# Inverse of the 16-blocks in a two-layer trunk: DRAM trips moved from the SP queue to Pool's queue, forward substitution moved from VectorE to Pool

## The chip, the cores and the metric

The kernel runs on one core of one Trainium2 chip. The metric is the device time of one execution in microseconds (us). PE is TensorE, DVE is VectorE, ACT is ScalarE, POOL is GpSimd, SP is SyncE; SPq is the queue of DMAs that SP issues. Every engine works its own list of instructions in the order in which the program wrote them.

## The reference

Two layers, each of three sub-layers on 256 rows of width 1024: a SwiGLU feed-forward, a token-mixing sub-layer, a second SwiGLU feed-forward, each with shift, scale and gate from a conditioning vector. The mixing sub-layer runs a convolution module, causal attention of 6 heads and a gated DeltaNet of 6 heads side by side. Everything is float32.

What matters here is in the DeltaNet: for each head and each chunk of 64 rows a unit lower triangular system is solved.

```
L = jnp.where(strict, jnp.einsum('bhncd,bhnsd->bhncs', k_beta, k) * decay, 0.0)
T = lax.linalg.triangular_solve(eye + L, jnp.broadcast_to(eye, L.shape), left_side=True, lower=True)
u = T @ v_beta
w = T @ (k_beta * jnp.exp(g)[..., None])
```

## The kernel before

**Weights.** All weights (about 250 MB) stream through four 1 MB buffers called `raw`, loaded by SP in a fixed order (`dmas`, line 420). ACT casts each unit to a high part `hi`, DVE subtracts to get a low part `lo` (`convert`, line 503), and PE multiplies in three passes. The conditioning matrix is accumulated on DVE (`adaacc`, `Lb`).

**What sets the order.** Each engine's list is written at build time by a planner: the class `Clock` (line 80) keeps a modelled time for each engine and for the DMA queue, and generators in `sides` (line 1655) step forward from `tick` when their inputs should be ready on PE's modelled time. So a change of what runs where also changes the order of other work.

**The mixing sub-layer.** PE multiplies the projection units in turn: rotated queries and keys (`mqk`, banks copied to `Y` tiles), attention values (`mv`, 48 matmuls of 384 columns), the gate `gz`. Between them stand the matmuls of the side work: the DeltaNet's products (`PT`, `LD`), attention scores and softmax (`E`), and the inverse.

**The inverse** (`inverse`, line 1367) takes the diagonal 32-blocks of the 24 chunk matrices in `LD`. SP writes them to DRAM (`scr_l`, line 1266, four DMAs) and reads the 16-blocks back with one block per partition (`Lb`, line 1378, two DMAs), so that 96 partitions hold 48 pairs. DVE then does 15 steps of forward substitution, two instructions each (`T` and `W`, lines 1389 and 1391), and a transposing copy (line 1392). SP writes the result to DRAM (`scr_w`, line 1398, four DMAs) and reads it back in the layout for PE (`C`, tile `Wc`, line 1400, two DMAs). PE combines the 16-blocks to 32-blocks and then 64-blocks in a chain of small matmuls, each followed by copies on ACT or DVE (lines 1410 to 1480). The DeltaNet (`delta_rule`) needs the end of that chain.

**The taps.** The depthwise convolution has 31 taps for each of two blocks, 62 in a mixing. A tap is either one DVE instruction (`cacc<-hc,colB,cacc`) or an ACT multiplication into one of two `ctap` buffers and an addition on Pool (`cacc<-cacc,ctap`). `taps` (line 1522) chooses by the modelled times; while `cfg["lo_pool"]` is false, which is from line 1372 to line 1393, it uses DVE alone. `fill` (line 1514) puts taps into modelled holes of DVE.

`idle("gp")` (line 1067) is a condition for a side generator: it waits until Pool's modelled time is close to PE's.

Of the kernel before, what the change touches and what calls it, by code (L numbers as in the profile page):

```python
# [14 lines left out]
OP = mybir.AluOpType  # L15
# [64 lines left out]
class Clock:  # L80


    def __init__(self):
        self.t = dict(pe=0.0, act=0.0, dve=0.0, gp=0.0, dma=0.0)
        self.writes, self.reads, self.used, self.slots, self.free = {}, {}, {}, {}, {}
        self.table = None
        self.filler = None
# [45 lines left out]
    def note(self, engine, op, args, kw):  # L133
        if op == "preload_act_table_set":
            self.t["act"] += 1.28 if args[0] != self.table else 0.0
            self.table = args[0]
            return
        out = kw.get("out", args[0] if args else None)
        ins = [x for x in list(args[0 if "out" in kw else 1:]) + [v for k, v in kw.items() if k not in ("out", "accum_out")]
               if hasattr(x, "tensor")]  # L140
        name = out.tensor.name
        start = max([self.t[engine], self.free.get(name, 0.0), self.last(self.reads, out), engine != "dma" and self.ready(out)]
                    + [self.ready(x) + 0.1 for x in ins])
        filler = self.filler
        if engine == "dve" and filler:
            self.filler = None
            while start - self.t["dve"] > HOLE and filler():
                pass
            self.filler = filler
            start = max(start, self.t["dve"])  # L150
        if engine == "dma":
            n = self.size(out) * out.shape[0] * 4 / 360e3
            self.t["dma"] = start + n
            end = start + n + (4.5 if "scr_" in name + ins[0].tensor.name else 2.0)
        else:
            end = self.t[engine] = start + self.cost(engine, op, out, ins)
        for log, aps in ((self.writes, [out, kw.get("accum_out", out)]), (self.reads, ins)):
            for x in aps:
                lo, hi = (0, 1 << 40) if engine == "dma" and x is out else self.span(x)
                w = log.setdefault(x.tensor.name, [])  # L160
                w[:] = [y for y in w if not (lo <= y[0] and y[1] <= hi)] + [(lo, hi, end)]
                self.used[x.tensor.name] = max(self.used.get(x.tensor.name, 0.0), end)
# [15 lines left out]
def trunk(ctx, tc, t, out):  # L178
    nc = tc.nc
# [1 line left out]
    psum = ctx.enter_context(tc.tile_pool(name="ps", bufs=1, space=PSUM))  # L181
    ctx.enter_context(tc.manual_schedule())
    clock = Clock()
    act, dve, pe, gp, sp = (clock.engine(n, e) for n, e in (("act", nc.scalar), ("dve", nc.vector), ("pe", nc.tensor),
                                                            ("gp", nc.gpsimd), ("dma", nc.sync)))

    def sb(shape, tag, dt=F32, bufs=1):
        return clock.tile(tag, bufs, pool.tile(shape, dt, name=tag, tag=tag, bufs=bufs))
# [67 lines left out]
    p = ps([128, 128], "x")  # L256
# [749 lines left out]
    scr_l = nc.dram_tensor("scr_l", [12, 4, 32, 32], F32, kind="Internal").ap()  # L1006
    scr_w = nc.dram_tensor("scr_w", [2, 12, 4, 32, 32], F32, kind="Internal").ap()
    late = {}

    def mixing(l, G, normed, nxt):  # L1010
# [128 lines left out]
        LD = LT[:, :NH * 256].rearrange("p (h t x) -> p h t x", t=2, x=128)  # L1139
# [117 lines left out]
        def pairs():  # L1257
            yield from until("kh")
            for h in range(NH):
                yield from until(("decay", h))  # L1260
                yield (kh, PT[:, h])
                yield from products(h, kh)
            yield (LD,)
            for q in range(4):
                c = slice(32 * q, 32 * q + 32)
                sp.dma_start(out=scr_l.rearrange("g b j i -> b j g i")[q], in_=LD.rearrange("p h t x -> p (h t) x")[c, :, c])
            ev["LT"] = True
            yield from until("qh")
            for h in range(NH):
                yield (qh,)  # L1270
                yield from products(h, qh)
            ev["PT"] = True
# [84 lines left out]
        W = sb([96, 2, 16, 16], "W")  # L1357
# [9 lines left out]
        def inverse():  # L1367
# [7 lines left out]
            Um, X = (buf[:, o:o + 384].rearrange("p (m i) -> p m i", i=32) for o in (256, 640))  # L1375
            for i in range(2):
                c = slice(16 * i, 16 * i + 16)
                sp.dma_start(out=Lb[48 * i:48 * i + 48], in_=scr_l.rearrange("h b j i -> (h b) j i")[:, c, c])
            yield (LD,)
            LM = LD.rearrange("p h t x -> p (h t) x")  # L1380
            for q in QUAD:
# [2 lines left out]
            V = W[:, 0]  # L1384
            for j in range(15):
                n, ni = j + 1, 15 - j
                T = sb([96, 64], "T", bufs=2)
                T = T[:, :n * ni].rearrange("p (c i) -> p c i", i=ni)
                dve.tensor_tensor(T, V[:, 0:n, j:j + 1].to_broadcast([96, n, ni]),
                                 Lb[:, j:j + 1, n:16].to_broadcast([96, n, ni]), op=OP.mult)  # L1390
                dve.tensor_tensor(V[:, 0:n, n:16], V[:, 0:n, n:16], T, op=OP.subtract)
            dve.tensor_copy(W[:, 1], V.rearrange("p c i -> p i c"))
            cfg["lo_pool"] = True
            C = sb([128, 2, 12, 32], "Wc")
            for f in range(2):
                for i in range(2):
                    c = slice(16 * i, 16 * i + 16)
                    sp.dma_start(out=scr_w[f].rearrange("h b c i -> (h b) c i")[:, c, c], in_=W[48 * i:48 * i + 48, f])
            for f in (1, 0):
                sp.dma_start(out=C[:, f], in_=scr_w[f].rearrange("h b c i -> (b c) h i"))  # L1400
            yield from until("kh")
            wide = sb([128, 1536], "S6a")
            TA, X64 = (wide[:, o:o + 768].rearrange("p (m i) -> p m i", i=64) for o in (0, 768))
# [533 lines left out]
    for n, (l, ph) in enumerate(order):  # L1937
        nxt = None
        if n + 1 < len(order):
            nl, nph = order[n + 1]  # L1940
            nxt = ((nl, 3 * nph + 1), (nl, 3 * nph))

        def normed(after=(), scaled=False, norm=True, l=l, ph=ph, n=n, G=G):
            if n and norm:
                rstd()
            h = modulate_whole(G["gs"], need_mod(l, 3 * ph), after) if ph == 1 else \
                modulate(G["gs"], need_mod(l, 3 * ph), after, scaled)
            if n == 0:
                cfg["wide"] = ("x", "x")
            cfg["lo_pool"] = True  # L1950
            cfg["mixing"] = ph == 1
            return h

        if ph == 1:
            G = mixing(l, G, normed, nxt)
        else:
            G = ffn(l, 1 if ph == 0 else 2, G, normed, 2 if ph == 0 else 8, nxt)
        if n == 0:
            zero = sb([128, 384], "E", bufs=3)
            gp.memset(zero, 0.0)  # L1960
            for f in range(2):
                sp.dma_start(out=scr_w[f].rearrange("h b c i -> (h b c i)").rearrange("(p n) -> p n", n=384), in_=zero)
            dve.tensor_copy(negdb, late["neg"][:, 0])
            dve.tensor_copy(negsb, late["neg"][:, 1])
            dve.tensor_copy(gt, late["neg"][:, 2])
            side_dma.append(load_rows(1))
# [23 lines left out]
```

## Time and profile before

| | us |
|---|---|
| three runs | 1217.0, 1206.73, 1216.96 |
| median | 1216.96 |
| profiled execution, own time | 1213.49 |
| its span | 1211.7 |
| PE busy | 1139.0 (94%) |
| DVE busy | 895.1 (74%) |
| ACT busy | 621.0 (51%) |
| POOL busy | 132.9 (11%) |

The profiled execution is one run with the hardware profiler; its span is what the trace covers. Busy times do not count DMA issue or waits. The granted clock is given as a share of the full 2.4 GHz. The two mixings stand at about 235 to 440 us (layer 0) and 830 to 1010 us (layer 1).

### The profile page before, as it was taken

The numbers are of one execution on the slowest core, as the hardware profiler recorded it, in microseconds if no ns is written. First come the engines' busy times: TensorE is split into PE (matmuls) and PEld (weight loads), VectorE is DVE, ScalarE is ACT, GpSimd is POOL, SyncE is SP. The second block draws the span as 40 slices with busy tenths as digits, with TensorE's granted clock in tenths as the row PEclk, the third lists the DMA queues.
The fourth block names the chain that finished last, engine by engine and source line by source line (L and its number), as shares of the span: only waits on it lengthen the run. The fifth ranks groups of instructions, "written<-read, shape, count | busy, mean of one in ns | idle before, by whom it ended". The sixth has DMA issues, their size and how long they took to land.

```text
span 1211.7 us, 22081 instructions
## 1 busy us (share of the span) xinstructions
PE 1139.0 (94%) x9085; PEld 1060.6 (88%) x9085; DVE 895.1 (74%) x1364; ACT 621.0 (51%) x1061; POOL 132.9 (11%) x139
## 2 busy tenths in 40 slices
PE   5799999999798779999999999999989989999997
PEld 4799999878677779999999999997868779999996
DVE  5778877658886588878769887774879938866554
ACT  4364444447646455444446544444656656544443
POOL 0610000102420010000001000001027101000001
PEclk9899999999879889999999999999988989999999
DMA  8759888656261376979764997893543514786640
GB/s 318 243 197 327 310 297 316 178 169 192 58 205 37 108 240 216 322 262 338 256 229 166 328 323 257 294 295 93 174 149 72 176 56 154 260 262 224 178 155 35
DMA packets 185740, 256.52 MB, mean 212 GB/s; under 512 B 26704, under 2 KB 152744, under 8 KB 185640
## 3 DMA queue, kind: packets, MB, share of 16 engines
q1 hardware_dynamic: 185640, 255.12, 63.1%
q8 instruction: 71, 1.16, 0.4%
q14 instruction: 29, 0.24, 0.1%
HBM read 252.86 MB, written 2.23 MB: 211 GB/s over the span
## 4 chain that ended last, share of the span: by engine, by line
PE 74%; DVE 16%; ACT 6%; issue 2%; POOL 1%; DMA 1%; SPq 0%; POOLq 0%; ACTq 0%; DVEq 0%
PE pm L171 45%; PE pa L171 27%; DVE adaacc L171 3%; DVE lo L171 2%; DVE H L171 2%; PE px L171 2%; ACT hi L171 1%; DVE W L171 1%; DVE v L171 1%; ACT L171 1%; DVE T L171 1%; DVE cacc L171 1%; DVE tmp L171 1%; DVE mod L171 1%; DMA xin_LT<-in_x_dram 1%
## 5 line engine op out<-in xcount | busy, mean ns | idle before, releaser
L171 PE MATMUL pm<-H,hi 128*128 128x256 f32 x2816 | 505.8, 282 | 1.4 <-DVE H L171 1.2
L171 DVE TENSOR_TENSOR lo<-raw,hi 128x1024 fp32r<-128x1024 f32 (+1 forms) x300 | 361.7, 1227 | 109.8 <-ACT hi L171 109.6
L171 PEld LDWEIGHTS pm<-H,hi 128*128 128x128 f32 x2816 | 431.9, 189 | 4.0 <-DVE H L171 2.0
L171 ACT CAST hi<-raw 128x1024 fp32r<-128x1024 f32 (+1 forms) x306 | 312.3, 1042 | 211.0 <-PE pm L171 93.8
L171 PE MATMUL pm<-H,lo 128*128 128x256 f32 x1408 | 392.5, 281 | 1.3 <-DVE lo L171 1.3
L171 PEld LDWEIGHTS pm<-H,lo 128*128 128x128 f32 x1408 | 264.7, 189 | 1.7 <-DVE lo L171 1.7
L171 PE MATMUL pa<-Y,hi 128*128 128x256 f32 x1312 | 245.7, 290 | 11.9 <-ACT S3a L171 7.5
L171 PEld LDWEIGHTS pa<-Y,hi 128*128 128x128 f32 x1312 | 208.3, 196 | 14.8 <-ACT S3a L171 7.9
L171 PE MATMUL pa<-Y,lo 128*128 128x256 f32 x656 | 187.8, 286 | 0.0
L171 PEld LDWEIGHTS pa<-Y,lo 128*128 128x128 f32 x656 | 129.5, 197 | 0.0
L171 ACT CAST Y<-tmp 128x256 fp32r<-128x256 f32 x88 | 35.9, 408 | 131.5 <-DVE tmp L171 131.5
L171 POOL TENSOR_TENSOR xin_LT<-xin_LT 128x256 f32<-128x256 f32 x35 | 27.1, 774 | 648.7 <-ACT xin_LT L171 646.4
L171 DVE SCALAR_TENSOR_TENSOR adaacc<-raw,c_act,adaacc 128x1024 f32<-128x1024 f32 x70 | 93.9, 1342 | 1.6
L171 POOL TENSOR_TENSOR cacc<-cacc,ctap 128x256 f32<-128x256 f32 x68 | 60.5, 890 | 204.8 <-DVE cacc L171 155.8
L171 DVE SCALAR_TENSOR_TENSOR Lb<-raw,c_act,Lb 128x1024 f32<-128x1024 f32 x56 | 71.8, 1283 | 4.3 <-DMA raw<-in_w_ada_dram 3.1
L171 DVE TENSOR_TENSOR Y<-tmp,Y 128x256 fp32r<-128x256 f32 x88 | 37.5, 426 | 41.7 <-ACT Y L171 41.7
L171 PE MATMUL pm<-Y,raw 128*128 128x256 f32 x288 | 66.8, 384 | 0.0
L171 PEld LDWEIGHTS pm<-Y,raw 128*128 128x128 f32 x288 | 53.4, 190 | 8.9 <-issue 1.0
L171 ACT ACTIVATE tmp<-pm 128x256 f32<-128x256 f32 x84 | 31.8, 379 | 52.1 <-PE pm L171 52.0
L171 PE MATMUL pa<-hi,Y 128*128 128x512 f32 x176 | 54.8, 393 | 0.0
L171 DVE TENSOR_REDUCE mod<-px 128x4 f32<-128x512 f32 x34 | 23.4, 689 | 33.6 <-PE px L171 33.5
L171 ACT ACT_TABLE_LOAD x28 | 35.9, 1283 | 14.9 <-DVE v L171 13.8
(301 smaller groups left out, 1337.8 us busy)
## 6 DMA issues: line engine op xcount, KB each, us to landing
raw<-in_w_ada_dram SPq DMA_DIRECT2D x70, 1024.0 KB
raw<-in_ffn_w_gate_dram SPq DMA_DIRECT2D x44, 1024.0 KB
raw<-in_ffn_w_up_dram SPq DMA_DIRECT2D x44, 1024.0 KB
raw<-in_ffn_w_down_dram SPq DMA_DIRECT2D x44, 1024.0 KB
raw<-in_w_in_dram SPq DMA_DIRECT2D x12, 1024.0 KB
raw<-in_w_in_dram SPq DMA_DIRECT2D x20, 512.0 KB
raw<-in_w_out_dram SPq DMA_DIRECT2D x16, 512.0 KB
raw<-in_w_in_dram SPq DMA_DIRECT2D x4, 768.0 KB
```

Source lines behind the costliest of these rows:

```text
L171: return getattr(real, op)(*args, **kw)
```

## The change

All 12 DMAs of each inverse go from SP's list to Pool's list (`qd` is a second modelled queue whose DMAs are issued by Pool), and so do the two DMAs that once write zeros to `scr_w` after the first sub-layer. The 30 instructions of the substitution and the copy go from DVE to Pool, with a yield on `idle("gp")` after each step. The planner has a modelled time `dma2` for Pool's DMAs beside Pool's own `gp`.

```diff
-        self.t = dict(pe=0.0, act=0.0, dve=0.0, gp=0.0, dma=0.0)
+        self.t = dict(pe=0.0, act=0.0, dve=0.0, gp=0.0, dma=0.0, dma2=0.0)
...
-        if engine == "dma":
+        if engine.startswith("dma"):
             n = self.size(out) * out.shape[0] * 4 / 360e3
-            self.t["dma"] = start + n
+            self.t[engine] = start + n
             end = start + n + (4.5 if "scr_" in name + ins[0].tensor.name else 2.0)
...
-                sp.dma_start(out=scr_l.rearrange("g b j i -> b j g i")[q], in_=LD.rearrange("p h t x -> p (h t) x")[c, :, c])
+                qd.dma_start(out=scr_l.rearrange("g b j i -> b j g i")[q], in_=LD.rearrange("p h t x -> p (h t) x")[c, :, c])
...
-                sp.dma_start(out=Lb[48 * i:48 * i + 48], in_=scr_l.rearrange("h b j i -> (h b) j i")[:, c, c])
+                qd.dma_start(out=Lb[48 * i:48 * i + 48], in_=scr_l.rearrange("h b j i -> (h b) j i")[:, c, c])
...
-                dve.tensor_tensor(T, V[:, 0:n, j:j + 1].to_broadcast([96, n, ni]),
+                gp.tensor_tensor(T, V[:, 0:n, j:j + 1].to_broadcast([96, n, ni]),
                                  Lb[:, j:j + 1, n:16].to_broadcast([96, n, ni]), op=OP.mult)
-                dve.tensor_tensor(V[:, 0:n, n:16], V[:, 0:n, n:16], T, op=OP.subtract)
-            dve.tensor_copy(W[:, 1], V.rearrange("p c i -> p i c"))
+                gp.tensor_tensor(V[:, 0:n, n:16], V[:, 0:n, n:16], T, op=OP.subtract)
+                yield idle("gp")
+            gp.tensor_copy(W[:, 1], V.rearrange("p c i -> p i c"))
...
-                    sp.dma_start(out=scr_w[f].rearrange("h b c i -> (h b) c i")[:, c, c], in_=W[48 * i:48 * i + 48, f])
+                    qd.dma_start(out=scr_w[f].rearrange("h b c i -> (h b) c i")[:, c, c], in_=W[48 * i:48 * i + 48, f])
             for f in (1, 0):
-                sp.dma_start(out=C[:, f], in_=scr_w[f].rearrange("h b c i -> (b c) h i"))
+                qd.dma_start(out=C[:, f], in_=scr_w[f].rearrange("h b c i -> (b c) h i"))
...
-                sp.dma_start(out=scr_w[f].rearrange("h b c i -> (h b c i)").rearrange("(p n) -> p n", n=384), in_=zero)
+                qd.dma_start(out=scr_w[f].rearrange("h b c i -> (h b c i)").rearrange("(p n) -> p n", n=384), in_=zero)
```

The order of the instructions, at the places on which the prediction rests (layer 0; layer 1 reads alike):

Pool's list from the zero fill to the start of the substitution, as the difference:

```order
 L171 MEMSET E 128x384
+L171 DMA scr_w<-E 128x384 x2
 L171 TENSOR_TENSOR cacc<-cacc,ctap 128x256 x4
+L171 DMA scr_l<-xin_LT 32x12x32 x4
+L171 DMA Lb<-scr_l 48x16x16 x2
 L171 TENSOR_TENSOR Lb<-xin_LT,kc 32x384 x4
+L171 TENSOR_TENSOR T<-W,Lb 96x15
+L171 TENSOR_TENSOR W<-W,T 96x15
```

The first four additions of taps stay in front; behind them stand the trip's first half, then the four products for `Um` (line 1382), then the substitution, whose 30 rows follow one another.

Pool's list from the end of the substitution on, as the difference:

```order
+L171 COPY W<-W 96x256
+L171 DMA scr_w<-W 48x16x16 x4
+L171 DMA Wc<-scr_w 128x12x32 x2
 L171 MEMSET S6a 32x12x32
-L171 TENSOR_TENSOR cacc<-cacc,ctap 128x256 x30
+L171 TENSOR_TENSOR cacc<-cacc,ctap 128x256 x23
 L171 TENSOR_TENSOR xin_LT<-xin_LT 128x256 x21
```

All further additions of taps stand behind the whole trip; there are 23 instead of 30, so seven taps of each mixing are now DVE's (35 instead of 28).

ACT's list from the copy of the first rotated bank on, before:

```order
L171 COPY Y_3252<-pm_3117 128x512
L171 ACTIVATE ctap<-hc,colB 128x256
L171 CAST hi<-raw 128x768
L171 ACTIVATE ctap<-hc,colB 128x256 x7
L171 CAST hi<-raw 128x768
L171 ACTIVATE ctap<-hc,colB 128x256 x3
L171 COPY Y_3366<-pm_3254 128x512
```

and now:

```order
L171 COPY Y_3205<-pm_3117 128x512
L171 CAST hi<-raw 128x768 x2
L171 ACTIVATE ctap<-hc,colB 128x256
L171 COPY Y_3379<-pm_3207 128x512
L171 ACTIVATE ctap<-hc,colB 128x256
L171 CAST hi<-raw 128x768
L171 ACTIVATE ctap<-hc,colB 128x256 x3
L171 ACTIVATE E,sm<-pa_3338,mx 128x128
L171 ACTIVATE E,sm<-pa_3338,mx 128x256
L171 CAST hi<-raw 128x768
```

The multiplications for Pool's taps stand later and closer to other work: the third one needs a `ctap` buffer that Pool's first addition behind the trip gives back, and behind it wait the softmax of the first heads and the last cast for `mv`. Nine of them stand ahead of the instruction that normalises the first head's weights, 15 ahead of the copies of the attention values, which PE needs before the second use of `Wc`.

DVE's list where the substitution stood, now:

```order
L171 SCALAR_TENSOR_TENSOR Q_2761<-Q_2761,tmp_3016 128x512
L171 SCALAR_TENSOR_TENSOR cacc<-hc,colB,cacc 128x256 x3
L171 TENSOR_TENSOR lo<-raw,hi 128x768
L171 SCALAR_TENSOR_TENSOR cacc<-hc,colB,cacc 128x256 x2
L171 STREAM_SHUFFLE tmp_3239<-Y_3205 128x256 x2
L171 TENSOR_TENSOR tmp_3239<-tmp_3239,kc 128x512
L171 TENSOR_TENSOR Y_3205<-Y_3205,kc 128x512
L171 TENSOR_TENSOR Y_3205<-Y_3205,tmp_3239 128x512
L171 TENSOR_TENSOR PT<-pa_3231,PT 128x384
```

Five taps stand where the 31 instructions stood, and the `PT` products (which free PSUM banks for PE) come right behind the first rotation. On PE the first matmuls that read `Wc` stand behind 24 of the 48 `mv` matmuls instead of 36, and behind the scores of three heads instead of two; the transposition of the first head's weights stands six `mv` matmuls behind them. At the second use of `Wc` five heads have their scores instead of three, and DVE has 6 taps left behind it instead of 15. The output projection starts ahead of the DeltaNet's last copy.

## Rows read from the trace of the kernel before

**Rows 1.** The page: busy time of each engine (share of the span, instructions), and shares of the chain that ended last by engine.
```profile
PE 1139.0 (94%) x9085; PEld 1060.6 (88%) x9085; DVE 895.1 (74%) x1364; ACT 621.0 (51%) x1061; POOL 132.9 (11%) x139
PE 74%; DVE 16%; ACT 6%; issue 2%; POOL 1%; DMA 1%; SPq 0%; POOLq 0%; ACTq 0%; DVEq 0%
```

**Rows 2.** What PE waited for in the mixing of layer 0 (285 to 400 us, first three rows) and of layer 1 (877 to 995 us): total us, times, longest.
```profile
PE pa L171 <- ACT v L171: 4.9, 1, 4.9
PE pa L171 <- ACT S3a L171: 3.8, 1, 3.8
PE pa L171 <- DVE PT L171: 3.3, 1, 3.3
...
PE pa L171 <- DVE PT L171: 1.3, 1, 1.3
```

**Rows 3.** DVE in order of time, layer 0: start us, us, engine, instruction. From the substitution's first instruction to the products that PE waited for.
```profile
314.74 0.16 DVE L171 TENSOR_TENSOR T<-W,Lb 96x15 f32<-96x15 f32 x1
...
324.67 0.78 DVE L171 TENSOR_TENSOR T<-W,Lb 96x48 f32<-96x48 f32 x1
...
328.64 0.81 DVE L171 COPY W<-W 96x256 f32<-96x256 f32 x1
...
334.47 1.94 DVE L171 TENSOR_TENSOR PT<-pa,PT 128x384 f32<-128x384 f32 x4
```

**Rows 4.** Groups of DVE instructions over the whole run: count, busy us, mean ns of one, idle before.
```profile
L171 DVE SCALAR_TENSOR_TENSOR cacc<-hc,colB,cacc 128x256 f32<-128x256 f32 x52 | 24.9, 482 | 2.3 <-POOL cacc L171 1.2
L171 DVE TENSOR_TENSOR W<-W,T 96x15 f32<-96x15 f32 (+7 forms) x30 | 12.9, 430 | 1.0
L171 DVE TENSOR_TENSOR T<-W,Lb 96x15 f32<-96x15 f32 (+7 forms) x30 | 12.4, 412 | 1.0
```

**Rows 5.** Stretches of layer 0 (first three rows) and layer 1: us, busy of PE, PEld, DVE, ACT, POOL (instructions), granted clock, DMA share, GB/s.
```profile
331.80:335.10 3.30, 0.03 (x1) 0.04 (x1) 3.27 (x5) 1.97 (x4) 3.13 (x3) 0.95 0.56 88
335.10:351.40 16.30, 16.30 (x47) 12.85 (x48) 16.13 (x27) 6.93 (x11) 6.19 (x8) 0.50 0.45 129
...
390.00:400.00 10.00, 5.93 (x40) 5.22 (x39) 3.33 (x5) 6.70 (x11) 0.00 (x0) 0.81 0.00 0
...
926.50:942.00 15.50, 15.50 (x148) 12.36 (x149) 15.33 (x24) 8.43 (x14) 9.76 (x10) 0.67 0.43 115
```

**Rows 6.** SP's DMA issues in order of time, layer 0: start us, us, how many.
```profile
295.46 1.88 SPq L171 DMA_DIRECT2D scr_l<-xin_LT  x4
298.69 0.88 SPq L171 DMA_DIRECT2D Lb<-scr_l  x2
...
328.63 2.07 SPq L171 DMA_DIRECT2D scr_w<-W  x4
332.51 1.14 SPq L171 DMA_DIRECT2D Wc<-scr_w  x2
```

**Rows 7.** What SP's queue waited for, 290 to 345 us: total us, times, longest.
```profile
SPq L171 <- DVE W L171: 27.7, 1, 27.7
...
SPq L171 <- DMA scr_w<-W: 1.8, 1, 1.8
SPq L171 <- DMA scr_l<-xin_LT: 1.2, 1, 1.2
```

**Rows 8.** Pool in order of time (layer 0, last row layer 1): start us, us, instruction, count, idle time before and its releaser.
```profile
294.92 3.36 POOL L171 TENSOR_TENSOR cacc<-cacc,ctap 128x256 f32<-128x256 f32 x4 [52.46 <-DVE cacc L171]
298.25 4.62 POOL L171 TENSOR_TENSOR Lb<-xin_LT,kc 32x384 f32<-32x384 f32 x4
302.93 0.41 POOL L171 MEMSET S6a<- 32x384 f32 x1
...
890.47 4.62 POOL L171 TENSOR_TENSOR Lb<-xin_LT,kc 32x384 f32<-32x384 f32 x4
```

**Rows 9.** Prices on Pool. First row: the tap additions, ns min/median/max; the others: groups by shape with count, busy us, mean ns.
```profile
L171 POOL TENSOR_TENSOR cacc<-cacc,ctap x68: 722/745/1636, 294.9 to 969.3; 128x256 f32<-128x256 f32 x68
L171 POOL TENSOR_TENSOR cacc<-cacc,ctap 128x256 f32<-128x256 f32 x68 | 60.5, 890 | 204.8 <-DVE cacc L171 155.8 <-ACT ctap L171 17.6 <-DVE W L171 14.2
L171 POOL TENSOR_TENSOR lo<-raw,hi 128x1024 fp32r<-128x1024 f32 x6 | 16.8, 2809 | 39.2 <-ACT hi L171 39.2
L171 POOL TENSOR_TENSOR PT<-PT,rstd 128x256 f32<-128x256 f32 x8 | 12.4, 1584 | 0.0
L171 POOL TENSOR_TENSOR xin_LT<-raw,PT 128x512 f32<-128x512 f32 x3 | 4.0, 1317 | 179.5 <-DVE raw L171 179.5
```

**Rows 10.** ACT in order of time, layer 0: two multiplications for taps, the copy of the second rotated bank, two casts, four instructions that normalise softmax rows.
```profile
323.18 1.01 ACT L171 ACTIVATE ctap<-hc,colB 128x256 f32<-128x256 f32 x2
...
325.34 0.59 ACT L171 COPY Y<-pm 128x512 f32<-128x512 f32 x1 [0.22 <-PE pm L171]
...
335.58 1.98 ACT L171 CAST hi<-raw 128x1024 fp32r<-128x1024 f32 x2
...
363.23 1.49 ACT L171 ACTIVATE E<-E,sm 128x128 f32<-128x128 f32 x4
```

**Rows 11.** PE's first and second use of `Wc` in layer 0, and the second in layer 1.
```profile
352.31 1.02 PE L171 MATMUL pa<-Wc,Lb 32*32 32x32 f32 x96
363.00 0.92 PE L171 MATMUL pa<-Lb,Wc 32*32 32x32 f32 x69
...
951.41 0.92 PE L171 MATMUL pa<-Lb,Wc 32*32 32x32 f32 x69
```

More of the change, by code (lines that the diff above doesn't have):

```diff
@@ L141, in note @@
         name = out.tensor.name
-        start = max([self.t[engine], self.free.get(name, 0.0), self.last(self.reads, out), engine != "dma" and self.ready(out)]
+        start = max([self.t[engine], self.free.get(name, 0.0), self.last(self.reads, out), not engine.startswith("dma") and self.ready(out)]
                     + [self.ready(x) + 0.1 for x in ins])
@@ L158, in note @@
             for x in aps:
-                lo, hi = (0, 1 << 40) if engine == "dma" and x is out else self.span(x)
+                lo, hi = (0, 1 << 40) if engine.startswith("dma") and x is out else self.span(x)
                 w = log.setdefault(x.tensor.name, [])
@@ L183, in trunk @@
     clock = Clock()
-    act, dve, pe, gp, sp = (clock.engine(n, e) for n, e in (("act", nc.scalar), ("dve", nc.vector), ("pe", nc.tensor),
-                                                            ("gp", nc.gpsimd), ("dma", nc.sync)))
+    act, dve, pe, gp, sp, qd = (clock.engine(n, e) for n, e in (
+        ("act", nc.scalar), ("dve", nc.vector), ("pe", nc.tensor), ("gp", nc.gpsimd), ("dma", nc.sync), ("dma2", nc.gpsimd)))
     def sb(shape, tag, dt=F32, bufs=1):
```

## The prediction

> **What bounds the kernel now.** I read the page first. PE is busy 94% of the span and makes up 74% of the chain that ended last; DVE follows with 16%, and Pool does almost nothing (11% busy, 1% of the chain) [rows 1]. So time is won only where PE stands still or runs slowly, and the change touches the two mixings alone. Next I listed what PE waited for there. Layer 0 has three waits above 3 us, and one is the change's target: 3.3 us for DVE's `PT` products; in layer 1 the same wait is 1.3 us [rows 2]. DVE's own list in order of time shows why: the substitution holds DVE from 314.74 to 328.64 us, and the products, which give PE its banks back, come only at 334.47 [rows 3]. An instruction of the substitution takes 0.16 us alone at the start and 0.78 us once Pool's additions run beside it [rows 3]; the means are 0.41 and 0.43 [rows 4].
>
> The stretches show the second half of the price. Behind the 3.3 us hole the granted clock is 0.50 for 16.3 us, which is the lower level of 1.2 GHz, and in layer 1 the mean is 0.67 over 15.5 us [rows 5]. At full clock the same work would have taken 8.2 us less in layer 0 and 5.1 us less in layer 1 (0.33 of 15.5).
>
> **What the change can win.** Hole and slow clock together are 3.3 + 8.2 = 11.5 us in layer 0 and 1.3 + 5.1 = 6.4 us in layer 1: **17.9 us**. A further 3.8 us per mixing is the wait for ACT's last copy of the DeltaNet [rows 2], which the new order covers with the output projection: 25.5 us at the very most, so no result below about 1188.
>
> DVE loses 62 instructions in all, 60 of them 12.9 + 12.4 = 25.3 us [rows 4], and gains 14 taps of 0.482 us, 6.7 us [rows 4]. That saving is worth what PE waits for DVE, which is in the 17.9 us already; I count nothing more for it.
>
> SP's queue stood 27.7 us behind the substitution with weight loads waiting [rows 7]. I price its release at zero: at 390 to 400 us the DMA share is 0.00 [rows 5], so the loads had caught up long before the mixing's end, and no wait on a weight load is among PE's [rows 2]. The two zero fills go to Pool into an idle stretch of 52 us [rows 8]: zero too.
>
> **What it costs: Pool's list becomes one long chain.** Everything from the first DMA to the last now stands in one list, and the remaining additions of taps stand behind it. Call g the time that Pool needs for one DMA and s for one instruction of the substitution. In layer 0 Pool is free of its first four additions at 298.25 [rows 8]. Then:
>
> - four `scr_l` DMAs, 4g; they land 1.2 us later (SP's wait for the same trip) [rows 7];
> - two `Lb` DMAs, 2g; the four `Um` products, 4.62 us [rows 8], which cover the landing;
> - 30 s, then the copy of 256 elements, 0.72 us by Pool's shortest addition of that size [rows 9];
> - four `scr_w` DMAs, 4g, their landing 1.8 us [rows 7], two `Wc` DMAs, 2g.
>
> 298.25 + 1.2 + 4.62 + 0.72 + 1.8 = 306.6, so Pool is through at R = 306.6 + 30 s + 12 g.
>
> For s: Pool's shortest addition with 256 elements takes 0.72 us, with 512 the mean is 1.32 us [rows 9], which is 2.3 ns an element and 0.13 us besides. The 15 steps have 680 elements, 45 on average, so 0.23 us is the lower end. The upper end is 0.78 us, an instruction that waits for its neighbour on the other engine [rows 3]. I take 0.42, the mean that these instructions have on DVE beside Pool [rows 4]: 12.6 us, bounds 7 to 23.
>
> For g the trace of before has no Pool DMA. Lower end: SP issues these twelve in 1.88 + 0.88 + 2.07 + 1.14 = 5.97 us [rows 6], 0.50 us each. Upper end: Pool's slowest instruction by mean, 2.81 us [rows 9]. The DMAs consist of 384 (`scr_l`), 768 (`Lb`, `scr_w`) and 1536 (`Wc`) runs, 9216 in all. If Pool works through a run as through an element, g is 768 x 2.3 ns + 0.13 = 1.9 us on average; I take that, because it is the one row-based price that grows with the work, and the ends lie about as far on both sides. 12 g = 22.8.
>
> So R is 306.6 + 12.6 + 22.8 = **342** in layer 0 and, from 890.47 [rows 8] by the same sum, **934** in layer 1. `Wc` lands about 1.8 us later, at 344 and 936. Without the hole PE would reach its first use of `Wc` 11.5 us before 352.31 [rows 11], near 340: it waits 4 us there.
>
> **Who waits for Pool.** ACT is the worse case. It reaches its third new `ctap` soon after the copy of the second bank, which ends at 325.9 [rows 10], so near 327; the buffer is given back by Pool's first addition, behind a memset of 0.41 us [rows 8], at about R + 1.3 = 343. ACT stands 16 us, and behind it the first softmax, the last `mv` cast and with that DVE's `lo`. After R the list resumes at Pool's pace: nine additions of 0.89 us [rows 9] stand ahead of the first head's weights, R + 9 at the earliest, and PE waits for those again. PE's second use of `Wc` stands behind the copies of the attention values. Up to those ACT's list holds 15 `ctap` of 0.5 us, five casts of up to 1.0 and about a dozen pieces of 0.4 [rows 10], some 17 us from R + 1.3 on; 24 matmuls follow. So the second use comes at R + 22, my estimate: 364 against 363.00, and 956 against 951.41 [rows 11]. That is +1 and +5 us.
>
> Behind that point the new order has 9 fewer DVE taps per mixing (9 x 0.482 = 4.3 us [rows 4]) and no 3.8 us wait; I credit half of the 8.1, and take as much back for the clock behind PE's new waits, half of what the hole of before cost. Net zero.
>
> **Sum.** 1 + 5 = +6 us on the profiled execution's 1213.5: 1219.5, **forecast 1219**. That execution lies 3.5 us under the median of 1216.96, inside the spread of the runs shown (1206.7 to 1217.0), so I give no further correction. In g the sum is 6 + 24 (g - 1.9): no change at g = 1.65, a percent faster at 1.15, a percent slower at 2.15. One percent (12 us) is about what a measurement of this kernel can tell from no change.
>
> **Rivals.**
>
> *Pool's DMAs are cheap.* With g at 0.9, not twice SP's 0.50 [rows 6], R is 330 and 922, ACT hardly stands, and the sum is 6 - 24 = -18: **1195**. For it: SP's row, and Pool's idle time. Against: the runs are many, and Pool's time grows with its elements [rows 9]. It decides below g = 1.15. The Trainium skill (DMA: Bandwidth & Descriptors, section on the anatomy of one DMA) says that most of the about 2 us of a Pool DMA is the receipt of its write and that "You can emit a lot of descriptors before the incremental cost shows up", and gives about 1 us to the first byte (section on latency). By that 1 us the sum, an estimate, would be 1198; no run here shows it yet.
>
> *Pool's DMAs are dear.* With g at the upper end, 2.8 us, R is 353 and 945, and ACT, DVE and PE all stand behind the trip in each mixing: 6 + 22 = +28, **1241**. It decides from g = 2.15 on. For it: Pool's list has nothing to hide the DMAs behind. Against: no row shows a DMA at that price.
>
> *The substitution is slow on Pool.* It would be so if each of its instructions waited for a neighbour on DVE: 0.23 + one tap of 0.48 [rows 4] = 0.71 us, 30 x 0.29 = 9 us more per mixing: **1237**. For it: the Pool products that ran beside DVE's long accumulations took 1.58 us, against 0.745 for an addition of that size [rows 9]. Against: the tap additions among the substitution now keep a median of 0.745, so beside short neighbours Pool hardly waits. The Trainium skill (SBUF — State Buffer, Who interferes with whom) says that an instruction of DVE with two SBUF inputs and a Pool instruction that reads SBUF exclude each other, whichever starts first winning; by it the 1237 would hold wherever DVE's taps start first, and the 0.78 us of [rows 3] agrees with it for the other order.
>
> *The change relieves nothing*, because the planner fills DVE's hole with taps: five stand there now, 2.4 us instead of 14, so the order speaks against it; it gets no chance of its own.
>
> **Chances.** Forecast (g between 1.15 and 2.15) 0.37, cheap DMAs 0.30, dear DMAs 0.23, slow substitution 0.10. Faster by over 1% is the cheap case, 0.30; within 1% 0.37; slower the last two, 0.33. The forecast's own range is 1207 to 1231. For 8 in 10 I go from 1193, just under the cheap case, to 1249, beyond the dear case with a slower substitution; the rest of the bounds lies outside.
>
> **What the next profile would show.** Right: no substitution on DVE, `PT` products before 328, the 3.3 us wait gone; Pool's twelve DMAs near 23 us per mixing and its last one ending near 342; ACT waiting for `cacc` around 327 to 343; PE waiting before `Wc` and before the first head's transposition. Wrong: Pool through before 333 (then it is faster), or after 350; a PE wait on weights; or the second use of `Wc` far from R + 22, which is the softest number here.

## The result, and the profile after

| | before | after |
|---|---|---|
| median of 9 runs | 1213.69 us | **1201.89 us** |
| ratio, 95% interval | | **0.9896**, 0.9872 to 0.9919 |
| profiled execution, its span | 1213.49, 1211.7 us | 1202.57, 1200.8 us |

The change makes the kernel one percent faster. The forecast was 1219, no change: 17 us too high, though the wide range of 1193 to 1249 holds the time.

The page of after: busy times, and shares of the chain that ended last.

```profile
PE 1130.7 (94%) x9085; PEld 1052.0 (88%) x9085; DVE 874.4 (73%) x1314; ACT 612.6 (51%) x1049; POOL 169.3 (14%) x213
PE 71%; DVE 12%; ACT 6%; POOL 6%; issue 3%; DMA 1%; SPq 0%; POOLq 0%; DVEq 0%; ACTq 0%
```

Against [rows 1], 20.7 us of DVE's work are gone, and Pool is now 6% of the chain: the trip has become part of what bounds the kernel. PE has the same 9085 matmuls; its busy time is 8.3 us less, at a mean granted clock of 0.976 instead of 0.965, and the span less that busy time is 2.6 us less. Pool's list in layer 0, in order of time (idle time before and its releaser in brackets):

```profile
298.93 2.48 POOL L171 DMA_DIRECT2D scr_l<-xin_LT  x4
305.68 1.46 POOL L171 DMA_DIRECT2D Lb<-scr_l  x2 [4.27 <-PE pa L171]
307.15 4.45 POOL L171 TENSOR_TENSOR Lb<-xin_LT,kc 32x384 f32<-32x384 f32 x4
311.67 0.28 POOL L171 TENSOR_TENSOR T<-W,Lb 96x15 f32<-96x15 f32 x1
...
326.22 0.61 POOL L171 COPY W<-W 96x256 f32<-96x256 f32 x1
326.77 2.92 POOL L171 DMA_DIRECT2D scr_w<-W  x4
332.26 2.07 POOL L171 DMA_DIRECT2D Wc<-scr_w  x2 [2.56 <-DMA scr_w<-W]
334.31 0.44 POOL L171 MEMSET S6a<- 32x384 f32 x1
334.69 3.98 POOL L171 TENSOR_TENSOR cacc<-cacc,ctap 128x256 f32<-128x256 f32 x5
```

The twelve DMAs take 2.48 + 1.46 + 2.92 + 2.07 = 8.93 us, 0.74 each; the substitution 326.22 - 311.67 = 14.55 us, 0.485 an instruction. Pool is through at R = 334.3. (The wait before `Lb` is for the landing of `scr_l`: in layer 1 the same wait, 3.45 us, is put down to that DMA, and the row's `PE pa` here is the profile's guess.) ACT in order of time shows who pays:

```profile
326.39 0.51 ACT L171 ACTIVATE ctap<-hc,colB 128x256 f32<-128x256 f32 x1
326.80 0.82 ACT L171 CAST hi<-raw 128x768 fp32r<-128x768 f32 x1
335.46 0.51 ACT L171 ACTIVATE ctap<-hc,colB 128x256 f32<-128x256 f32 x1 [7.84 <-POOL cacc L171]
```

ACT stands 7.84 us for its third new `ctap` (9.89 in layer 1), and PE behind it. What PE waited for in the mixing of layer 0 (first three rows) and of layer 1:

```profile
PE pa L171 <- ACT E L171: 6.7, 4, 4.7
PE pa L171 <- ACT V L171: 2.1, 1, 2.1
PE pa L171 <- ACT v L171: 2.0, 1, 2.0
...
PE pa L171 <- ACT E L171: 8.1, 3, 6.4
PE pa L171 <- ACT v L171: 2.0, 1, 2.0
PE pm L171 <- issue: 1.6, 1, 1.6
```

The waits of [rows 2] for `PT` (3.3 and 1.3 us) and for `S3a` (3.8 each) are gone, that for `v` has fallen from 4.9 to 2.0, and in their place stands the softmax `E`. In sum PE hardly waits less. Where the 10.9 us between the two spans came from is seen when the mixing is cut at three of PE's instructions: the one behind the wait for `v`, the second use of `Wc`, and the one behind the wait for `mod` after the mixing (in layer 1, behind the wait for `xT`).

| PE, us | before | after | difference |
|---|---|---|---|
| layer 0, start of span to `v` | 310.1 | 307.6 | -2.5 |
| `v` to second use of `Wc` | 52.9 | 55.1 | +2.2 |
| second use to `mod` | 55.8 | 46.5 | **-9.2** |
| `mod` of layer 0 to `v` of layer 1 | 483.6 | 480.2 | -3.3 |
| `v` to second use | 49.1 | 55.6 | **+6.5** |
| second use to `xT` | 61.3 | 56.2 | -5.1 |
| `xT` to the end | 199.0 | 199.6 | +0.6 |

The two stretches of layer 0 as windows (us; busy of PE, PEld, DVE, ACT, POOL; granted clock; DMA share; GB/s), before:

```profile
310.10:363.00 52.90, 49.62 (x357) 42.38 (x357) 45.93 (x89) 29.78 (x58) 23.15 (x27) 0.80 0.41 122
363.00:418.76 55.76, 45.61 (x592) 38.60 (x591) 31.88 (x64) 33.59 (x77) 3.03 (x3) 0.91 0.23 77
```

and after:

```profile
307.56:362.62 55.06, 46.75 (x364) 38.41 (x364) 42.91 (x78) 29.20 (x66) 42.59 (x63) 0.94 0.34 102
362.62:409.15 46.53, 40.71 (x584) 34.95 (x584) 28.03 (x50) 30.49 (x63) 2.60 (x3) 1.00 0.33 111
```

In the last stretch PE idles 10.2 us before and 5.8 after, and the clock is 1.00 instead of 0.91. Before, PE stood 3.8 us there for ACT's `S3a`, the DeltaNet's last copy [rows 2], and the clock was 0.74 right behind that wait:

```profile
397.47:408.00 10.53, 10.53 (x65) 9.61 (x66) 3.61 (x5) 3.51 (x5) 0.00 (x0) 0.74 0.31 100
```

After, the output projection covers that copy: the wait is gone and the clock stays at 1.00. Of the kernels below, those with the lists of before have this wait (3.1 to 3.8 us), and those with the lists of after don't. Not all of the 9.2 us is won, for the new order also moves work: the scores, weights and products of two more heads now stand ahead of the second use of `Wc` and 18 matmuls of the gate behind it. By the busy times 41.56 and 45.22 of two kernels below (*old order on Pool* and *substitution only*), with the clock at 0.96 in both, that lengthens the middle by 3.7 us. So it is the sum of the two stretches that counts: -7.0 us in layer 0 and +1.4 in layer 1. The middle has the hole's slow clock repaired (0.80 to 0.94) and is longer all the same, by that work and by what PE waits behind ACT.

The stretches that end at `v` give 2.5 + 3.3 = 5.8 us, more than half of the 10.9. Their gain has a source that the prediction does not have: DVE's products for `H` (count, ns min/median/max), before and after.

```profile
L171 DVE TENSOR_TENSOR H<-Y,H x8: 428/1076/1235, 295.5 to 301.9; 128x256 fp32r<-128x256 f32 x8
```

```profile
L171 DVE TENSOR_TENSOR H<-Y,H x8: 411/416/946, 296.2 to 300.2; 128x256 fp32r<-128x256 f32 x8
```

Before, `Um` started on Pool at 298.25 [rows 8] and ran beside the last four of the eight; now it stands behind the landing of `scr_l`, at 307.15. These four take 0.41 us each instead of 1.21 to 1.24, together 3.2 us less. (Three of the others run beside Pool's additions in both kernels and take 0.94 us in both, so the medians in the rows mix cases.)

### The profile page after: what moved, and what is told of

The parts are those of the page before. It is cut to its first block, busy times and chain, and to the rows that moved or that the text cites. A ratio compares the mean times of both kernels' runs of the same rounds, so it can differ in the third digit from the quotient of the medians.

```text
span 1200.8 us, 22053 instructions
## 1 busy us (share of the span) xinstructions
PE 1130.7 (94%) x9085; PEld 1052.0 (88%) x9085; DVE 874.4 (73%) x1314; ACT 612.6 (51%) x1049; POOL 169.3 (14%) x213
## 4 chain that ended last, share of the span: by engine, by line
PE 71%; DVE 12%; ACT 6%; POOL 6%; issue 3%; DMA 1%; SPq 0%; POOLq 0%; DVEq 0%; ACTq 0%
PE pm L171 45%; PE pa L171 25%; DVE lo L171 3%; DVE adaacc L171 3%; PE px L171 2%; ACT hi L171 1%; POOL W L171 1%; POOL cacc L171 1%; POOL T L171 1%; POOL Lb L171 1%; DVE mod L171 1%; ACT L171 1%; DVE tmp L171 1%; DVE Lb L171 1%; DVE Y L171 1%
## 5 line engine op out<-in xcount | busy, mean ns | idle before, releaser
L171 DVE TENSOR_TENSOR lo<-raw,hi 128x1024 fp32r<-128x1024 f32 (+1 forms) x300 | 362.1, 1226 | 131.8 <-ACT hi L171 131.3
L171 PE MATMUL pa<-Y,hi 128*128 128x256 f32 x1312 | 241.3, 286 | 4.5 <-DVE xT L171 4.5
L171 PEld LDWEIGHTS pa<-Y,hi 128*128 128x128 f32 x1312 | 204.1, 192 | 6.7 <-DVE xT L171 5.3
L171 POOL TENSOR_TENSOR cacc<-cacc,ctap 128x256 f32<-128x256 f32 x54 | 52.3, 973 | 122.0 <-DVE cacc L171 112.8
L171 DVE SCALAR_TENSOR_TENSOR cacc<-hc,colB,cacc 128x256 f32<-128x256 f32 x66 | 36.0, 562 | 10.3 <-POOL cacc L171 9.4
```

Source lines behind the costliest of these rows:

```text
L171: return getattr(real, op)(*args, **kw)
```

## Experiments

Three things changed at once: the DMAs' **queue**, the **engine** of the substitution, and the **order** that the planner wrote because of it. The first four kernels keep one or the other. "The lists of before" (or of after) means that PE, DVE and ACT have that order.

**DMAs only.** The substitution goes back to DVE, and the lists are those of before.

```diff
-                gp.tensor_tensor(T, V[:, 0:n, j:j + 1].to_broadcast([96, n, ni]),
+                dve.tensor_tensor(T, V[:, 0:n, j:j + 1].to_broadcast([96, n, ni]),
...
-                yield idle("gp")
-            gp.tensor_copy(W[:, 1], V.rearrange("p c i -> p i c"))
+            dve.tensor_copy(W[:, 1], V.rearrange("p c i -> p i c"))
```

> All fourteen DMAs on Pool's queue, the substitution back on DVE; the lists of PE, DVE and ACT are those of before. Theory Q (Um stands behind the landing of scr_l in Pool's list, so DVE's eight H products run without a neighbour): PE's wait for v falls from 4.9 to 2.0 us in both mixings, worth 7 us with the clock behind it. Theory S (the gain is the substitution's leaving DVE): the PT wait stays at 3 us, and since Pool's 30 additions now stand behind the scr_w DMAs, which wait for DVE's W, ACT stands too: 1214 to 1225. Theory W (the gain is SP's queue, free for weights): all of the gain, 1202. Q and S together: 1206 to 1216.

Measured 1.0109 (1.0084 to 1.0134): slower, at 1226 us just above what theory S expected. The wait for `v` is 2.0, as in after, and the `PT` wait that theory S expected is not there; but Pool's additions wait for DVE's `W`, ACT for them (13.8 us at one place in layer 0, 15.5 in layer 1), PE for ACT. PE's waits, layer 0, then layer 1:

```profile
PE pm L171 <- ACT Y L171: 8.4, 1, 8.4
...
PE pm L171 <- ACT Y L171: 10.2, 1, 10.2
```

The queue alone loses; theory W falls.

**Substitution only**, and **second half on SP**. In the first all DMAs go back to SP, in the second only `scr_w`, `Wc` and the zero fills; both keep the lists of after.

```diff
-                    qd.dma_start(out=scr_w[f].rearrange("h b c i -> (h b) c i")[:, c, c], in_=W[48 * i:48 * i + 48, f])
+                    sp.dma_start(out=scr_w[f].rearrange("h b c i -> (h b) c i")[:, c, c], in_=W[48 * i:48 * i + 48, f])
...
-                qd.dma_start(out=C[:, f], in_=scr_w[f].rearrange("h b c i -> (b c) h i"))
+                sp.dma_start(out=C[:, f], in_=scr_w[f].rearrange("h b c i -> (b c) h i"))
```

> The substitution on Pool, all DMAs back on SP; the lists of PE, DVE and ACT are those of after. Pool no longer waits for a landing: the substitution starts near 303, ends near 318, ACT does not stand for ctap. Theory S with Q: the 4.7 and 6.4 us that PE waits for E go, with the slow clock behind them some 16 us, but Um runs beside the H products again and the v wait is back at 4.9 us, some 8 us: 1190 to 1198. Theory W: SP's queue stands behind W again, so the gain is gone: 1211 to 1215.

> After, with the second half of the trip (scr_w, Wc and the zero fills) back on SP's queue; the lists of PE, DVE and ACT are those of after. Pool's additions start near 327 instead of 334, 7.5 us earlier, since its list no longer holds the scr_w issue (2.9), its landing (2.6) and the Wc issue (2.1). Theory S with Q: ACT does not stand 7.8 us, PE's waits for E shrink to below 2 us, the v wait stays at 2.0: 1186 to 1194. Theory W: SP stands behind W from 307 to 327 again, half of the gain is lost: 1205 to 1210.

Measured 0.9853 (0.9831 to 0.9876) and **0.9788** (0.9766 to 0.9810), both as expected by S with Q, though SP's queue stands behind `W` for 24.1 us in the second. There Pool's first addition starts right behind the substitution:

```profile
324.42 0.62 POOL L171 COPY W<-W 96x256 f32<-96x256 f32 x1
324.99 0.41 POOL L171 MEMSET S6a<- 32x384 f32 x1
325.36 5.10 POOL L171 TENSOR_TENSOR cacc<-cacc,ctap 128x256 f32<-128x256 f32 x5
```

That is 9.3 us earlier than in after, 7.9 counted from PE's `v` (306.17 and 307.56). No stand of ACT for `ctap` is longer than 1.4 us, and the time falls by 13 us by the ratios (0.0108 x 1213.7): 1.7 us per us of R.

**First half only.** The kernel before with only `scr_l` and `Lb` on Pool's queue.

> Before, with only the six DMAs of the trip's first half (scr_l, Lb) on Pool's queue; the lists of PE, DVE and ACT are those of before, and the second half stays on SP. Theory Q: Um starts near 307 instead of 298, H takes 4.4 us instead of 7.6, the v wait falls by 2.9 us in each mixing and the slow stretch behind it gets shorter: 1205 to 1208. Theories S and W: nothing, 1212 to 1215.

Measured 1.0059 (1.0017 to 1.0102), at 1221 us above both expectations. The wait for `v` did fall to 2.0, but 5.6 us of PE's time went at the next place, a wait for `lo`, which stands behind the substitution on DVE. Its instructions (count, ns min/median/max):

```profile
L171 DVE TENSOR_TENSOR T<-W,Lb x15: 164/755/791, 311.5 to 329.7; 96x15 f32<-96x15 f32 x2, 96x28 f32<-96x28 f32 x2, 96x39 f32<-96x39 f32 x2, 96x48 f32<-96x48 f32 x2
```

Pool's additions, earlier now too, run beside nearly all of it: 18.5 us instead of 13.9. **Copy on Pool** makes them wait:

```diff
-            dve.tensor_copy(W[:, 1], V.rearrange("p c i -> p i c"))
+            nc.gpsimd.tensor_copy(W[:, 1], V.rearrange("p c i -> p i c"))
```

> The kernel with the first half of the trip on Pool and the substitution on DVE, with one change: the substitution's last copy stands on Pool, so Pool's additions wait for the substitution instead of running beside it; the lists of PE and ACT are the same. Theory N (an instruction of the substitution on DVE costs 0.2 us alone and 0.77 beside Pool's additions): 30 of them take 7 us instead of 18.5, the lo wait of 5.6 us and the PT wait of 2.1 go, ACT stands some 7 us for its third ctap instead: 1193 to 1205. Rival (the substitution's place on DVE is what costs, whoever runs beside it): 1214 to 1224.

```profile
L171 DVE TENSOR_TENSOR T<-W,Lb x15: 166/204/221, 312.7 to 319.4; 96x15 f32<-96x15 f32 x2, 96x28 f32<-96x28 f32 x2, 96x39 f32<-96x39 f32 x2, 96x48 f32<-96x48 f32 x2
```

The price that theory N gave holds: 0.20 us instead of 0.76, 7 instead of 18.5 us, and the waits for `lo` and `PT` go. The time does not: 0.9997 (0.9967 to 1.0026), 7.5 us under the kernel without that copy, but with a median of 1216 us in the rival's 1214 to 1224 and not in the 1193 to 1205 expected. ACT stands 7.2 us for its `ctap`, and the clock from `v` to the second use of `Wc` is 0.80, as in before. A quick substitution on DVE and a short wait for `v` together are worth nothing against before with its lists and this stand of ACT. That pointed to the order.

**A dose on Pool**: after, with the substitution's last copy 16 times more.

```diff
+            for _ in range(16):
+                nc.gpsimd.tensor_copy(W[:, 1], V.rearrange("p c i -> p i c"))
             gp.tensor_copy(W[:, 1], V.rearrange("p c i -> p i c"))
```

> After, with the last copy of the substitution issued 16 times more on Pool: 9.6 us more ahead of the scr_w DMAs in each mixing, the lists of PE, DVE and ACT those of after. Theory R (the end hangs on the moment at which Pool is through with the trip, two mixings, one for one, slope 2 us per us as between after and the kernel with the second half on SP): 1202 + 19 = 1221, 1216 to 1226, and PE's waits for E grow by 9 us each. Rival (ACT's stand in after is slack that other work covers): 1202 to 1208.

```profile
324.20 12.55 POOL L1394 COPY W<-W 96x256 f32<-96x256 f32 x16
```

Measured 1.0109 (1.0063 to 1.0154), by the ratios 25.9 us above after. The dose was 12.55 us per mixing, not 9.6; 25.9 / 12.55 is 2.06 us per us of R. Theory R holds.

**Um first** and **Um last** move the four `Um` products in Pool's list: ahead of the `Lb` DMAs in the kernel with the second half on SP, and behind the substitution in the one with all DMAs on SP.

> The kernel with the second half of the trip on SP, with the four Um products ahead of the Lb DMAs in Pool's list, so that they run while scr_l lands; all other lists the same. Pool is through 3 to 4 us earlier. Theory R with its slope of 2: 1178 to 1182. Rival (with the second half on SP nobody waits for Pool any more, the slope has ended): 1184 to 1189.

> The kernel with all DMAs on SP and the substitution on Pool, with the four Um products behind the substitution in Pool's list. Theory Q: the H products have no 384-element product beside them, only the first small instructions of the substitution; PE's wait for v falls from 4.9 to 2 to 3 us, and the substitution starts near 301: 1183 to 1189. Rival (the substitution's instructions hold DVE up as the products did): the v wait stays at 4.9, 1192 to 1197.

Measured 0.9790 (0.9759 to 0.9821) and 0.9768 (0.9737 to 0.9799). The first brings nothing against 0.9788: no ACT stand behind the trip is left to shorten, and `Um`, now at 301.9, runs beside two of DVE's taps ahead of `v`, which take 1.13 us each, so the wait for `v` is 3.3. The second has `v` at 2.0 and lands where it was expected: `H` ends at 299.6, before the substitution starts at 301.2, and the eight taps beside the substitution's first instructions take 0.50 us each, hardly more than their 0.482 [rows 4].

**Order and engine apart.** In *new order on DVE* and *old order on Pool* the substitution is written into the planner's clock for one engine and issued on the other; all DMAs on SP.

```diff
+    sub = clock.engine("gp", nc.vector)
...
-                gp.tensor_tensor(T, V[:, 0:n, j:j + 1].to_broadcast([96, n, ni]),
+                sub.tensor_tensor(T, V[:, 0:n, j:j + 1].to_broadcast([96, n, ni]),
```

> All DMAs on SP, the lists of PE and ACT those of after, and the 31 instructions of the substitution issued on DVE, at the places at which the planner of after had them for Pool. Theory O (the gain is the new order: the stretch from PE's second use of Wc to the wait for mod takes 46.5 us in it and 55 to 58 in the order of before, whichever queue the DMAs have): Pool is quiet, the substitution costs DVE 6 to 8 us that it has to spare: 1188 to 1200. Theory S (the gain is the engine): the PT hole is back and with it the loss, 1205 to 1216.

> Before, with the 31 instructions of the substitution issued on Pool and nothing else: all DMAs on SP, the lists of PE and ACT those of before, DVE's list that of before without them. Theory S: PT comes before 328, the 3.3 and 1.3 us holes and the slow clock behind them go: 1190 to 1200. Theory O: the holes go, but ACT stands behind Pool for its ctap and the stretch behind the second use of Wc keeps its 55 us: 1205 to 1215.

> The DMAs and the substitution on Pool as in after, but in the order of before (the lists of PE and ACT are those of before). If the queue's price is ACT's stand behind the trip, it is paid in full here, since in this order ACT meets its third ctap near 314 and the copy of the second rotated bank stands behind ten of them: Pool's additions start near 334, PE waits for that copy 12 us and more per mixing, 1225 to 1240. If instead the new order brought nothing, and engine and queue alone made after what it is: 1200 to 1206.

> The DMAs on Pool and the order of after, but the substitution's instructions issued on DVE at the places at which after has them for Pool. It ends near 330 on DVE, spread between other work, so Pool is through with the trip near 337 instead of 334. By the slope of 2 us per us, 1205 to 1212. If the engine of the substitution were worth anything by itself in this order: over 1215. If it is the order alone that pays: 1200 to 1204.

The last two, with all DMAs on Pool's queue, complete the cube (ratio to before):

| | old order, DVE | new order, DVE | old order, Pool | new order, Pool |
|---|---|---|---|---|
| DMAs on SP | 1 (before) | 0.9862 (0.9828 to 0.9895) | 0.9869 (0.9828 to 0.9910) | 0.9853 (0.9831 to 0.9876) |
| DMAs on Pool | 1.0109 (1.0084 to 1.0134) | 0.9933 (0.9908 to 0.9957) | 1.0149 (1.0087 to 1.0212) | 0.9896 (after) |

The first two have medians of 1201.2 and 1201.8 us where before, measured beside them, had 1218.3; by their ratios and the 1213.7 of the result that is 1197 and 1198, so the order alone gives what theory O expected of it, and the engine alone what theory S expected. Of the last two, the one with the old order is at 1234, as expected if the queue's price is paid in full, and the one with the new order at 1205, at the edge between two expectations. On SP order and engine each bring 1.3 to 1.4%, and together hardly more: the intervals leave room for half a percent, as do the profiled spans (1196.8 and 1197.4 against 1192.2 for both). The windows show why the two don't add. *Old order on Pool*, from `v` to the second use of `Wc` and on to `mod`:

```profile
310.46:352.02 41.56, 41.56 (x357) 36.08 (x357) 34.48 (x54) 29.66 (x58) 32.97 (x41) 0.96 0.44 121
352.02:410.94 58.92, 49.39 (x592) 41.55 (x591) 33.80 (x69) 33.65 (x77) 3.02 (x3) 0.86 0.28 96
```

and *new order on DVE*:

```profile
311.02:362.50 51.48, 46.47 (x364) 38.68 (x364) 46.62 (x109) 29.31 (x66) 22.35 (x21) 0.93 0.37 107
362.50:409.05 46.55, 40.79 (x583) 35.03 (x584) 28.04 (x50) 30.50 (x63) 2.61 (x3) 1.00 0.33 112
```

The engine wins the middle stretch (52.9 to 41.6: PE does not stand in it at all, and the clock is 0.96 instead of 0.80), and 3 us go again in the last, where the clock is 0.86. The order wins the last (55.8 to 46.6) and 1.4 us in the middle, in spite of the moved work. From `v` to `mod` before takes 108.7 us, the engine alone 100.5, the order alone 98.0, both (*substitution only*) 94.2: 14.5 us less, not 8.2 + 10.7 = 18.9. In the new order most of the engine's gain is already had, since its middle stretch has no wait for `PT` with the substitution on DVE either, and with both PE waits for ACT instead.

With the DMAs on Pool's queue, as in the change, the engine is worth little: 1.0149 against 1.0109 in the old order, where PE waits 12.4 and 15.0 us for the rotated copy, and 0.9896 against 0.9933 in the new. The order is worth 1.8% on DVE and 2.5% on Pool there, and with it the queue costs 0.7 and 0.4% instead of 1.1 and 2.8%. So **of the three things changed it is the order that makes after faster and not slower**: in the old order the same queue and engine lose 1.5%. Not all that after gains against before is the order's, though. The 5.8 us ahead of `v` come with the queue: the wait for `v` is 4.9 us where `Um` runs beside `H` (before, *substitution only*, *new order on DVE*, *old order on Pool*) and 2.0 in all other kernels but *Um first*, whatever the order. The last stretch takes 46.5 to 47.4 us in every kernel of this section up to here that has the lists of after, and 54 to 60 us in those with the lists of before.

**What is left.** *Told* and *held back* keep all DMAs on Pool and change the planner alone: its clock of Pool moves along with those DMAs, or Pool gets taps again only when `Wc` has landed.

```diff
             self.t[engine] = start + n
+            if engine == "dma2":
+                self.t["gp"] = max(self.t["gp"], start + n)
```

```diff
-            cfg["lo_pool"] = True
             C = sb([128, 2, 12, 32], "Wc")
...
             yield (Um, C)
+            cfg["lo_pool"] = True
```

> After, with one line more in the planner: its clock of Pool moves along with the DMAs on Pool's queue, so that it knows of the trip. All DMAs stay on Pool. If ACT's stand is the planner's blindness, it now gives DVE the taps of that time, ACT stands below 2 us instead of 7.8: 1186 to 1195. Rival (the order, not the stand, sets the end, and any other order loses the tail that after has): 1200 to 1215.

> After, with one line moved: Pool gets taps again when Wc has landed in the planner's time instead of when the substitution is through. All DMAs stay on Pool. As for the kernel before it: 1186 to 1195 if ACT's stand goes and nothing else comes; 1200 to 1215 if the taps that DVE then takes, or another order of PE, cost as much.

*Told* gives 0.9913 (0.9880 to 0.9946), inside the rival's range: ACT's longest stand is 1.3 us in layer 0, as meant, and 4.4 in layer 1, with as many taps on DVE as in after; but the order it writes takes 56.0 us from the second use to `mod`, with the clock at 0.82. *Held back* gives **0.9714** (0.9670 to 0.9759), 1184 us, the fastest kernel here by its median ratio. ACT waits 0.5 us for Pool between 305 and 365, and the middle stretch, with as many matmuls as in after (364), takes 44.5 us instead of 55.1:

```profile
307.47:352.00 44.53, 44.43 (x364) 37.13 (x364) 39.48 (x80) 22.09 (x49) 24.45 (x45) 0.96 0.45 135
```

ACT's not standing is only one part of this. DVE now has 12 more taps in each mixing, ACT's work in this stretch is 22.1 us instead of 29.2, and behind the second use PE has another order than after. No run takes these parts from one another.

Two more put the second half, or all DMAs with `Um` last, back on SP in that kernel.

> The kernel that gives Pool taps only when Wc has landed, and with it the second half of the trip (scr_w, Wc, zero fills) on SP; the lists of PE, DVE and ACT are those of that kernel. Its ACT does not stand for Pool, so Pool's being through 7 us earlier brings only what PE waits for Wc (1.3 us in one layer): 1181 to 1184. If the two gains add, 1170 to 1176.

> The kernel that gives Pool taps only when Wc has landed, with all DMAs on SP and the Um products behind the substitution; the lists of PE, DVE and ACT are those of that kernel. As for the kernel before it: the v wait stays at 2 us, the Wc wait goes: 1180 to 1184; 1170 to 1176 if the gains add.

Measured 0.9723 (0.9680 to 0.9765) and 0.9725 (0.9681 to 0.9769), both as expected: no further gain. Where ACT does not stand behind the trip, the queue costs nothing that these runs can tell.

## Why the prediction was wrong

**Right:** that Pool's list becomes one chain and that R decides, through ACT's third `ctap`; its slope of 2 us per us (2.06 and 1.7 measured); that the `PT` hole goes and a wait of PE before the first head's softmax comes; SP's release at zero; the zero fills at zero.

**The step that failed: "Net zero" behind the second use of `Wc`.** Behind it I had 8.1 us of possible gain in each mixing, credited half, and took that half back for the clock behind new waits. Measured are -9.2 and -5.1 us. The 3.8 us wait for `S3a` went in full, and with it the slow clock behind it (0.74 over 10.5 us in layer 0). The new waits lie ahead of that point, and the clock behind it is 1.00 in layer 0; in layer 1 it is 0.50 behind a wait of 1.6 us, and the gain is less:

```profile
949.40:959.70 10.30, 10.30 (x84) 8.10 (x85) 7.13 (x18) 4.29 (x14) 0.00 (x0) 0.50 0.01 2
```

Some of the two numbers is work that the new order moves ahead of the point, up to 3.7 us by the busy times above, which I had left out as well. In the trace nine taps of DVE start behind the second use, not the six that I read from the lists.

**A second term, put at nothing: the wait for `v`.** I priced what Pool's own instructions suffer beside DVE and not what DVE suffers beside `Um`, though the `v` wait stood first in [rows 2]. The wait fell by 2.9 us in each mixing, and the stretches that end there by 2.5 and 3.3.

**Right by luck: +1 and +5 us up to the second use.** Measured are 362.62 against 363.00, -0.4, and in layer 1, where after starts 9.6 us earlier, 944.95 + 9.6 against 951.41, +3.1; without what is gained at `v` that is +2.2 and +6.5. These are near the forecast because several sizes missed and cancelled. g was put at 1.9 us and is 0.74, near the lower bound: the price per run was taken from Pool's price per element, and 384, 768 and 1536 runs cost 0.62, 0.73 and 1.03 us. s was 0.42, measured 0.485. The landings were 1.2 and 1.8 by SP's rows, and are 4.3 and 2.6. R = 334.3 instead of 342. Against that, the second use came at R + 28, not R + 22: the moved work stands ahead of it, and beside the pieces that I had counted, ACT waits behind R another 3.4 us for Pool's additions and 2.9 for DVE's `mx`. The wait of 4 us that I expected at the first use of `Wc` is not there (0.4 us in layer 1). With g at 0.74 the formula 6 + 24 (g - 1.9) gives -22, that is 1192: the cheap rival's side, 10 us below what was measured. The condition of the cheap rival, g below 1.15, came true, but ACT stood all the same.

**A range that does not follow.** By the same formula g from 1.15 to 2.15 gives 1201 to 1225, and not the 1207 to 1231 that I wrote for the forecast's own range, which is the forecast and one percent on each side.

**Two prices.** Pool needs 0.62 us to issue a DMA of 384 runs and 1.03 for 1536. The Trainium skill (DMA: Bandwidth & Descriptors, anatomy of one DMA) says that many descriptors can be emitted before their cost shows; the rows agree as to the size, with a cost of 0.41 us for 1152 more runs that does show. DVE's `T` takes 0.20 us alone and 0.76 beside Pool's additions, which is its own time and most of an addition's 0.745 [rows 9]. The Trainium skill (SBUF — State Buffer, Who interferes with whom) says that the two exclude each other; the rows agree, and here the larger loss was DVE's: 18.5 us instead of 7 for the substitution there, against at most 14.7 instead of 12.3 on Pool.

## What to carry to other kernels

Where a planner writes the lists, a change of engine is two changes; take them apart by issuing on one engine what the planner books on another, before crediting either. When an engine takes over a serial chain with waits in it, look first at what shares its list and holds buffers that a third engine needs: here the moment at which two buffers came free set the price, 2 us for each us in two mixings. Keeping the other work off that engine until the chain was through was worth as much as moving the DMAs back, though these runs do not part it from the new order that came with it. A neighbour on DVE and Pool costs both: price it in both directions.

## What the hardware showed

- The same 30 instructions of 15 to 64 elements take 7 us on DVE with a quiet Pool, 13.9 in before and 18.5 with Pool's additions beside all of them; on Pool they take 12.3 to 14.7 us. So by itself DVE is the faster place.
- On Pool's queue the first half landed 3.0 to 4.3 us after its issue where SP waited 1.2 to 1.5, the second 2.5 to 4.9 where SP waited 1.7 to 2.2 in most kernels and up to 3.4. Weight loads were under way in some of these stretches, and no run tells the queue's share from theirs.
- The two zero fills of 128 long rows each took 0.65 us to issue on Pool's queue, no less than `scr_l` with 384 short ones, so the price does not follow the runs alone.
